# A ring of twenty weight buffers: the two that hold the normalized rows move from the ninth and tenth place to the nineteenth and twentieth

## The chip, the cores and the metric

The kernel runs on one core of one Trainium2 chip. The metric is the device time of one execution in microseconds (us); lower is better. The core's engines are PE (matrix products; PEld is its weight load), DVE (vector), ACT (scalar), POOL (GpSimd) and SP, which here only issues DMAs. Each engine works off its own list of instructions in order and waits on semaphores that other engines and landing DMAs raise.

## The reference, cut

An encoder layer on 512 rows of 1024 values: normalization, one projection, three groups of attention heads, an output projection with residual (`x` below), then a mixture of 32 experts. The part that matters here is the end:

```python
t = rms_norm(x, g_ffn)                        # the normalized rows, 512 x 1024
group = argmax(t @ w_r1 + b_r1)               # 1 of 4 groups
e0, e1 = top2((t @ w_r2 + b_r2)[group])       # 2 of its 8 experts, with gates
for every row and each of its two experts e:
    a = silu(t @ w1[e]) * (t @ w3[e])         # w1, w3: 32 x 1024 x 512
    y = a @ w2[e]                             # w2: 32 x 512 x 1024
    x += gate * y
```

Everything is float32. The three stacks of expert weights are 64 MiB each, 192 MiB in all, and the kernel reads every one of them once.

## The kernel before

**Stages.** By the profile's clock (us from the start of the span) the attention takes the time up to about 330. The output projection and the router follow: `route()` adds the residual (`x1`), normalizes it (`xr`, L1146), finds each row's experts, and makes one-hot tables that say which row goes to which slot of which expert. The experts run from 395 to the end, in 16 pairs `pr`: expert `pr` on 64 columns of PE, expert `pr + 16` on the other 64.

**The normalized rows.** `xr` lies in two buffers of 1 MiB, of the kinds `k0` and `va`, which attention has used before (L1144). ACT writes them row block by row block, stores each block to DRAM (`xd`, L1149), and PE reads them twice: for the first half of pair 0's gathered rows in `route()` (L1242), and for the second half in `gather_first` (L1389), which stands between the first two and the third of pair 0's products. Pairs 1 to 15 take their rows from `xd` by an indirect DMA that POOL issues (`rows_load`, L1361), two pairs ahead.

**The weights.** They come in 192 loads of 1 MiB, numbered 0 to 191 here, in the order in which PE uses them: per pair four of `w1`, four of `w3`, four of `w2` (names `w0_`, `w1_`, `w2_`; in pair 0 the order is `w1`, `w3`, `w1`, `w3` in twos). `load_w` (L926) takes the next one, picks a buffer, and puts a DMA on SP's list (L946 for `w1` and `w3`, L948 for `w2`). Load n waits until the readers of what lay in its buffer before are done. There are 20 buffers, in the order of `RING` (L36), and load n takes `RING[n % 20]`: so from load 20 on each load takes the place of the one 20 before it, and the first 20 take the places of things that attention or the router used:

- loads 0 to 7: `k2 b q k1 h h g g`
- loads 8 and 9: `k0` and `va`, the normalized rows
- loads 10 and 11: `m m`, the attention's output, read by the first half of the output projection
- loads 12 and 13: `h h`, split weights of the output projection (`wob`)
- loads 14 to 17: `d e j k`, laid where the other split weights (`wp`) and the rest of the attention's output (`mixb`) were
- loads 18 and 19: `v w`, laid where the router's temporaries (`val`, `tT`, `scr`) were

SP's list is worked off in order, so a load that waits holds all loads behind it. Beside its buffer, a load waits for the landing of an earlier DMA on the same one of eight semaphores (DMAHW0 to DMAHW7), which the stores of ACT share; this keeps about eight loads in flight.

**What sets the order around the change.** Calls of `load_w` are strewn through the program: eight loads late in the output projection (L1313, L1315), four behind `route()` (L1327), four when the `d e j k` buffers exist (L1334), two at L1449, then two in each half product (L1411) and in each half of the second product (L1502). Where a call stands sets only its place on SP's list; when it runs is set by what it waits for.

Of the kernel before, what the change touches and what calls it, by code (L numbers as in the profile page):

```python
# [32 lines left out]
F = 512  # L33
EPS = 1e-6
NEG = -1e30
RING = "k2 b q k1 h h g g k0 va m m h h d e j k v w".split()  # L36
LN_EXP = [s.name for s in SETS].index("natural_log_exp_and_others")

NA_KEYS = ((64, 248), (0, 248), (0, 248), (0, 192))
# [5 lines left out]
def tile_encoder(ctx: ExitStack, tc, x, mem, g_mix, g_mem, g_ffk, w_in, w_kv, w_out, gains,  # L45
# [35 lines left out]
    def granule(kind, name, dt=F32):  # L81
        return big.tile([P, 4, 512], dt, name=name, tag=kind, bufs=BUFS[kind])
# [17 lines left out]
    def pt(name):  # L100
        pts[0] += 1
        return bank("pt", NPT, name)
# [656 lines left out]
    def rows_turn(a):  # L759
        q = [bank(f"lg{j}", 1, "rT") if a % 2 else pt("rT") for j in range(2)]  # L760
        for k in range(KT):
            nc.tensor.transpose(q[k // 4][:, k % 4 * P:(k % 4 + 1) * P], x_sb[:, a, k * P:(k + 1) * P], ident)
        return q
# [109 lines left out]
    q = pt("warm")  # L873
# [12 lines left out]
    q = rows_turn(0)  # L886
# [32 lines left out]
    def rows_of(t):  # L919

        return t.rearrange("p (a b) c -> p a (b c)", b=2)

    def w2_rows(e):
        return w2[e].rearrange("(p k) c -> p k c", k=4)

    def load_w(count=1):  # L926
        for _ in range(count):
            n = loaded[0]
            if n >= len(order):
                return  # L930
            loaded[0] += 1
            pr, w, q, h = order[n]
            e = pr + 16 * h
            kind = RING[n % len(RING)]
            if kind in BUFS:
                t = granule(kind, f"w{w}_{e}_{q}")
            else:
                t = rings[kind].tile([P, 4, 512], F32, name=f"w{w}_{e}_{q}", tag="ring" + kind, bufs=RING.count(kind))
            wt[pr, w, q, h] = t
            if w == 1 and pr == NPAIR - 1 and q == 1:  # L940

                for k in (0, 2) if h else ():
                    for i in range(2):
                        nc.sync.dma_start(wt[pr, w, q, i][:, k:k + 2], w3[pr + 16 * i].rearrange("(p k) c -> p k c", k=KT)[:, 4 + k:6 + k, :])
            elif w < 2:
                nc.sync.dma_start(t, (w1, w3)[w][e].rearrange("(p k) c -> p k c", k=KT)[:, 4 * q:4 * q + 4, :])  # L946
            elif pr < NPAIR - 1:
                nc.sync.dma_start(rows_of(t), w2_rows(e)[:, 2 * q:2 * q + 2, :])  # L948
            elif n < len(order) - 2:
                nc.sync.dma_start(t, w2_rows(e)[:, :, q * 512:(q + 1) * 512])  # L950
            elif n == len(order) - 1:
                for f, c in ((slice(0, 4), 0), (slice(0, 2), 256), (slice(2, 4), 256)):
                    for i in range(2):
                        nc.sync.dma_start(wt[pr, w, q, i][:, f, c:c + 256], w2_rows(pr + 16 * i)[:, f, 512 + c:512 + c + 256])
# [346 lines left out]
    for n in range(2):  # L1301
        for a in range(4):
            def products():
                wo_products(a, n, (4, 5, 6, 7))
                join(wo_post(a, n, pos[n], False))

            def before():
                for w, k in (((1, 4 + a),), ((0, a), (1, a)))[n]:
                    wo_split(w, k)
                if a == 3 and n == 0:  # L1310
                    load_wo(1, 0)
                if a == 2 and n == 1:
                    load_w(4)  # L1313
                if a == 3 and n == 1:
                    load_w(4)  # L1315
            until(ready((4, 5, 6, 7)))
            step(products, before)
# [6 lines left out]
    until(lambda: not active)  # L1324
    assert not soft_q and not out_q
    route()
    load_w(4)  # L1327
    keep.close()
    moe = ExitStack()
    ring_ = moe.enter_context(tc.tile_pool(name="ringd", bufs=1, reuse_waits="tile"))  # L1330
# [240 lines left out]
    with tc.If(flag > 0):  # L1571
        with tc.tile_pool(name="ov", bufs=1) as ov, tc.tile_pool(name="ovps", bufs=1, space=PS) as ovs:
            with tc.For_i(0, NE) as e:
# [6 lines left out]
                for a in range(4):  # L1580
# [7 lines left out]
                    for k in range(KT):  # L1588
                        q = ovs.tile([P, P], F32, name="ovq1")
# [12 lines left out]
                    for f in range(4):  # L1602
                        q = ovs.tile([P, P], F32, name="ovq1")
# [76 lines left out]
```

## Time and profile before

| what | us |
|---|---|
| median of 3 runs | 896.99 (895.33 to 898.39) |
| the profiled execution | 897.9, of which the span is 896.1 |
| PE busy in the span | 823.3 (92%) |
| DVE, ACT, POOL busy | 421.1, 256.6, 149.9 |

The span reaches from the first to the last instruction; 1.8 us lie around it. PE is busy nearly all the time in attention and most of the time in the experts; what it waits for there is in the rows below. Times of loads and waits are of this one execution.

### The profile page before, as it was taken

Reading aid. Unit: us, or ns where it says so; the run is one execution under the profiler, and the core shown is the slowest. Engines: PE = TensorE matmul, PEld = TensorE weight load, DVE = VectorE, ACT = ScalarE, POOL = GpSimd, SP = SyncE. Lnnn points to the kernel's source line nnn. Section 1 sums busy time; section 2 is a strip of 40 time slices with the busy share of each in tenths; the row PEclk is TensorE's granted clock in tenths of the full one; section 3 lists DMA queues with packets and bytes.
Section 4 is the critical chain, followed back from the end, with each engine's and each line's share of the span. In section 5 each row is a group of like instructions: output and inputs, shape, how many; then the busy total and the mean of one; then the engine's idle time right before and its main releaser. Section 6 shows DMA issues by size and latency. Waiting matters only on the chain. (4 is left out here: it accounts for less than half of the span.)

```text
span 896.1 us, 12694 instructions
## 1 busy us (share of the span) xinstructions
PE 823.3 (92%) x4758; PEld 517.8 (58%) x4758; DVE 421.1 (47%) x1200; ACT 256.6 (29%) x768; POOL 149.9 (17%) x150
## 2 busy tenths in 40 slices
PE   8799999999899999989898889889988998899996
PEld 7789889889688767855244324333443343244433
DVE  6787795348678666551133213312331333033315
ACT  4667666664445533510000000000000100010010
POOL 5454222333323232130000000000000000000000
PEclk8999999999999999979999999999999999999998
DMA  9233121131312567116999999999999999999994
GB/s 326 51 94 102 52 91 50 48 115 48 95 44 92 133 227 304 72 50 244 423 403 427 426 425 425 427 426 426 427 426 426 425 426 426 426 427 426 426 407 155
DMA packets 66209, 243.54 MB, mean 272 GB/s; under 512 B 9498, under 2 KB 34074, under 8 KB 42336
## 3 DMA queue, kind: packets, MB, share of 16 engines
q1 hardware_dynamic: 55376, 230.18, 63.7%
q10 hardware_dynamic: 8608, 8.55, 3.4%
q0 software_dynamic: 2160, 3.96, 1.2%
q8 instruction: 39, 0.64, 0.3%
q14 instruction: 26, 0.21, 0.1%
HBM read 242.31 MB, written 4.26 MB: 275 GB/s over the span
## 5 line engine op out<-in xcount | busy, mean ns | idle before, releaser
L1408 PE MATMUL h<-w,xT 128*64 128x512 f32 x1024 | 248.2, 604 | 41.7 <-DMA w<-in_w_dram 40.2
L1408 PEld LDWEIGHTS h<-w,xT 128*64 128x64 f32 x1024 | 81.7, 138 | 203.1 <-issue 115.2
L1475 DVE TENSOR_TENSOR u<-u,h 128x512 f32<-128x512 f32 x16 | 11.0, 689 | 246.6 <-PE h L1408 246.6
L1494 PE MATMUL y<-w,uT 128*64 128x512 f32 x480 | 106.7, 595 | 0.7 <-ACT uT L1482 0.7
L189 POOL TENSOR_TENSOR wp<-wc,wp 128x512 fp32r<-128x512 f32 x51 | 67.0, 1318 | 129.9 <-ACT wp L188 104.1
L232 PE MATMUL pj<-wp,hTh 128*128 128x256 f32 (+1 forms) x268 | 79.3, 296 | 0.7 <-ACT hTh L776 0.7
L1361 POOL DMA_INDIRECT rows<-xd,where x15 | 15.1, 1009 | 381.0 <-PE uTp L1480 235.7
L233 PE MATMUL pj<-wp,hTh 128*128 128x256 f32 (+1 forms) x268 | 76.8, 287 | 0.8 <-POOL wp L189 0.8
L234 PE MATMUL pj<-wp,hTl 128*128 128x256 f32 (+1 forms) x268 | 76.7, 286 | 0.2 <-DVE hTl L779 0.2
L1426 DVE TENSOR_TENSOR x<-x,c 128x512 f32<-128x512 f32 x120 | 73.1, 682 | 2.8 <-PE c L1424 1.3
L1494 PEld LDWEIGHTS y<-w,uT 128*64 128x64 f32 x480 | 33.6, 137 | 65.8 <-issue 64.7
L1500 DVE SCALAR_TENSOR_TENSOR yl<-y,gate,yh 128x512 fp32r<-128x512 f32 x30 | 22.5, 750 | 80.8 <-ACT yh L1499 80.8
L1499 ACT ACTIVATE yh<-y,gate 128x512 fp32r<-128x512 f32 x30 | 20.6, 687 | 134.6 <-PE y L1494 133.5
L1482 ACT ACTIVATE uT<-uTp 128x512 f32<-128x512 f32 x16 | 9.6, 598 | 165.9 <-PE uTp L1480 165.9
L232 PEld LDWEIGHTS pj<-wp,hTh 128*128 128x128 f32 (+1 forms) x268 | 51.8, 193 | 3.7 <-issue 1.4
L233 PEld LDWEIGHTS pj<-wp,hTh 128*128 128x128 f32 (+1 forms) x268 | 51.8, 193 | 1.2 <-POOL wp L189 1.2
L234 PEld LDWEIGHTS pj<-wp,hTl 128*128 128x128 f32 (+1 forms) x268 | 51.7, 193 | 0.4 <-DVE hTl L779 0.4
L1464 ACT ACTIVATE u<-h 128x512 f32<-128x512 f32 x16 | 9.6, 597 | 140.8 <-PE h L1408 140.8
L1423 PE MATMUL c<-yh,ot 128*128 128x512 f32 x120 | 48.2, 402 | 0.0
L1424 PE MATMUL c<-yl,ot 128*128 128x512 f32 x120 | 46.9, 391 | 0.0
L232 PE MATMUL pj<-wq,hTh 128*128 128x256 f32 (+1 forms) x124 | 37.4, 301 | 2.8 <-ACT raw L279 2.8
L234 PE MATMUL pj<-wq,hTl 128*128 128x256 f32 (+1 forms) x124 | 35.6, 287 | 0.0
(319 smaller groups left out, 1440.9 us busy)
## 6 DMA issues: line engine op xcount, KB each, us to landing
w<-in_w_dram SPq DMA_DIRECT2D x188, 1024.0 KB, 19.6
wc<-in_w_in_dram SPq DMA_DIRECT2D x15, 1024.0 KB, 5.2
wo<-in_w_out_dram SPq DMA_DIRECT2D x4, 1024.0 KB, 5.0
w<-in_w_dram SPq DMA_DIRECT2D x6, 512.0 KB, 10.8
wc<-in_w_kv_dram SPq DMA_DIRECT2D x2, 1024.0 KB, 9.0
x<-in_x_dram ACTq DMA_DIRECT2D x4, 512.0 KB, 8.4
xd<-xr ACTq DMA_DIRECT2D x4, 512.0 KB
nab<-in_na_tab_dram ACTq DMA_DIRECT2D x8, 248.0 KB
```

The costliest lines, as they stand in the source:

```text
L189: (eng or nc.gpsimd).tensor_sub(dst[1], src, dst[0])
L232: nc.tensor.matmul(o, th, self.hi[k], start=(k == 0), stop=False)
L233: nc.tensor.matmul(o, th, self.lo[k], start=False, stop=False)
L234: nc.tensor.matmul(o, tl, self.hi[k], start=False, stop=(k == KT - 1))
L1361: nc.gpsimd.indirect_dma_start(out=rows_in[pr % 2], out_offset=None, in_=xd, in_offset=bass.IndirectOffsetOnAxis(ap=where_[:, pr:pr + 1], ...
L1408: nc.tensor.matmul(p[h * 64:(h + 1) * 64, :], xT[k // 4][:, k % 4, h * 64:(h + 1) * 64], wt[pr, w, q, h][:, k % 4, :], start=(k == 0), sto ...
L1423: nc.tensor.matmul(c, ot[:, a], yh, start=True, stop=False)
L1424: nc.tensor.matmul(c, ot[:, a], yl, start=False, stop=True)
L1426: V.tensor_add(sl, sl, c)
L1494: nc.tensor.matmul(y[h * 64:(h + 1) * 64, :], uT[:, f, h * 64:(h + 1) * 64], rows_of(wt[pr, 2, q, h])[:, f % 2, n * 512:(n + 1) * 512], st ...
L1499: nc.scalar.activation(yh, y, AF.Copy, scale=gate[:, pr:pr + 1])
L1500: V.scalar_tensor_tensor(yl, y, gate[:, pr:pr + 1], yh, op0=ALU.mult, op1=ALU.subtract)
```

## The change

The ring's order for loads 0 to 17 skips `k0` and `va`; they come as loads 18 and 19. From load 20 on the order repeats with a period of 20 as before, so each load still takes the buffer of the one 20 before it. The call behind `route()` puts two loads instead of four on SP's list.

```diff
-RING = "k2 b q k1 h h g g k0 va m m h h d e j k v w".split()
+RING = "k2 b q k1 h h g g m m h h d e j k v w".split()
+AGAIN = ["k0", "va"] + RING
...
-            kind = RING[n % len(RING)]
+            kind = RING[n] if n < len(RING) else AGAIN[(n - len(RING)) % len(AGAIN)]
...
     route()
-    load_w(4)
+    load_w(2)
```

The line numbers behind the first hunk grow by one (L948 becomes L949). SP's list, loads 8 to 19, before; in brackets the semaphores each waits for: PE_49, DVE_49, Activation_49 and Pool_49 are raised by the engines, DMAHWn_49 by landings. The first two rows are `k0` and `va`, the next two `m m`, then `h h`, `d e j k`, `v w`:

```order
L948 DMA w2_0_0_4995<-in_w2_dram 128x2048 [waits DMAHW2_49,DMAHW1_49,DMAHW5_49,PE_49,Activation_49]
L948 DMA w2_16_0_4997<-in_w2_dram 128x2048 [waits DMAHW4_49,DMAHW3_49,DMAHW6_49,PE_49,Activation_49]
L948 DMA w2_0_1_4999<-in_w2_dram 128x2048 [waits DMAHW7_49]
L948 DMA w2_16_1_5001<-in_w2_dram 128x2048 [waits DMAHW0_49]
L946 DMA w0_1_0_5011<-in_w1_dram 128x2048
L946 DMA w0_17_0_5013<-in_w1_dram 128x2048
L946 DMA w0_1_1_5015<-in_w1_dram 128x2048 [waits DVE_49]
L946 DMA w0_17_1_5017<-in_w1_dram 128x2048 [waits DMAHW5_49,DVE_49]
L946 DMA w1_1_0_5063<-in_w3_dram 128x2048 [waits DMAHW6_49]
L946 DMA w1_17_0_5065<-in_w3_dram 128x2048 [waits DMAHW7_49]
L946 DMA w1_1_1_5077<-in_w3_dram 128x2048 [waits DVE_49,DMAHW0_49,Activation_49,Pool_49]
L946 DMA w1_17_1_5079<-in_w3_dram 128x2048 [waits DMAHW1_49]
```

The same place in the changed kernel. The loads are the same, the buffers are not: the first two rows are now `m m`, then `h h`, `d e j k`, `v w`, and the last two are `k0` and `va`:

```order
L949 DMA w2_0_0_4995<-in_w2_dram 128x2048 [waits DMAHW2_49,DVE_49]
L949 DMA w2_16_0_4997<-in_w2_dram 128x2048 [waits DMAHW3_49]
L949 DMA w2_0_1_5007<-in_w2_dram 128x2048 [waits DMAHW4_49,PE_49]
L949 DMA w2_16_1_5009<-in_w2_dram 128x2048 [waits DMAHW5_49,PE_49]
L947 DMA w0_1_0_5011<-in_w1_dram 128x2048 [waits DMAHW7_49,DVE_49,PE_49]
L947 DMA w0_17_0_5013<-in_w1_dram 128x2048 [waits DMAHW1_49,DVE_49,PE_49]
L947 DMA w0_1_1_5059<-in_w1_dram 128x2048 [waits DMAHW2_49,PE_49]
L947 DMA w0_17_1_5061<-in_w1_dram 128x2048 [waits DMAHW3_49,PE_49]
L947 DMA w1_1_0_5073<-in_w3_dram 128x2048 [waits DVE_49,PE_49,DMAHW5_49,Activation_49,Pool_49]
L947 DMA w1_17_0_5075<-in_w3_dram 128x2048 [waits DMAHW6_49,PE_49]
L947 DMA w1_1_1_5085<-in_w3_dram 128x2048 [waits DMAHW7_49,PE_49]
L947 DMA w1_17_1_5087<-in_w3_dram 128x2048 [waits DMAHW4_49,DMAHW0_49,PE_49]
```

What moved is the pair of waits on `xr`'s readers: from the head of this list to its end. Before, the ten loads behind it need hardly any wait of their own, because the wait at the head covers them; now each names the engine that last read its buffer.

The lists of PE, DVE, ACT and POOL hold the same instructions in the same order. On ACT, around the stores of the second and third block of `xr`, only semaphores differ. Before:

```order
L1149 DMA xd_61<-xr_4621 128x1024 [waits DMAHW2_49]
L1213 ACTIVATE scr_4726<-scr_4726 128x1 [waits DVE_49]
L1146 ACTIVATE xr_4769<-x1_4034,rst_4045 128x1024 [waits DVE_49]
L1149 DMA xd_61<-xr_4769 128x1024 [waits DMAHW3_49,Activation_49]
L1105 ACTIVATE junk_4784,sqs_4046<-x1_4034 128x512 [waits DVE_49]
```

And in the changed kernel:

```order
L1150 DMA xd_61<-xr_4621 128x1024 [waits DMAHW6_49]
L1214 ACTIVATE scr_4726<-scr_4726 128x1 [waits DVE_49]
L1147 ACTIVATE xr_4769<-x1_4034,rst_4045 128x1024 [waits DVE_49]
L1150 DMA xd_61<-xr_4769 128x1024 [waits DMAHW0_49,Activation_49]
L1106 ACTIVATE junk_4784,sqs_4046<-x1_4034 128x512 [waits DVE_49]
```

The stores stand where they stood; they share semaphores with other loads now (loads 5 and 7 here, load 10 for the fourth block), whose landing they wait for.

## Rows read from the trace of the kernel before

**Rows 1.** The page's span in 40 equal slices of 22.4 us: the busy share of the DMA engines in tenths, and GB/s moved.

```profile
DMA  9233121131312567116999999999999999999994
GB/s 326 51 94 102 52 91 50 48 115 48 95 44 92 133 227 304 72 50 244 423 403 427 426 425 425 427 426 426 427 426 426 425 426 426 426 427 426 426 407 155
```

**Rows 2.** SP's own waits between 326 and 480 us, longest first: line, what it waited for, us in total, times, longest.

```profile
SPq L948 <- PE xTp L1389: 36.2, 2, 35.7
SPq L948 <- DMA xd<-xr: 27.9, 1, 27.9
SPq L948 <- DMA gov<-wkb: 14.5, 1, 14.5
```

**Rows 3.** SP's timeline between 325 and 450 us: start, length of the merged stretch, issues in it.

```profile
326.62 20.81 SPq L946 DMA_DIRECT2D w<-in_w_dram  x8
411.09 2.29 SPq L948 DMA_DIRECT2D w<-in_w_dram  x4
413.43 12.79 SPq L946 DMA_DIRECT2D w<-in_w_dram  x8
429.03 19.61 SPq L948 DMA_DIRECT2D w<-in_w_dram  x4
```

**Rows 4.** Stretches of time: length, busy us of PE, PEld, DVE, ACT, POOL (instructions), granted clock of PE as a share of full, DMA share, GB/s.

```profile
354.00:358.00 4.00, 4.00 (x23) 2.81 (x22) 1.24 (x4) 0.84 (x3) 0.00 (x0) 1.00 0.99 412
358.00:362.00 4.00, 4.00 (x19) 3.29 (x18) 1.83 (x8) 2.08 (x5) 0.00 (x0) 1.00 0.07 29
366.00:370.00 4.00, 4.00 (x27) 3.48 (x24) 1.39 (x7) 2.45 (x7) 0.00 (x0) 1.00 0.00 0
406.00:410.00 4.00, 4.00 (x19) 4.00 (x18) 0.00 (x0) 0.00 (x0) 0.00 (x0) 1.00 0.00 0
414.00:418.00 4.00, 4.00 (x16) 1.18 (x14) 0.00 (x0) 0.00 (x0) 0.00 (x0) 0.76 1.01 422
440.00:480.00 40.00, 34.64 (x156) 13.51 (x156) 8.92 (x15) 2.57 (x4) 0.99 (x1) 1.00 1.00 412
520.00:560.00 40.00, 37.23 (x168) 14.70 (x166) 10.37 (x16) 3.94 (x6) 0.99 (x1) 1.00 1.01 426
```

**Rows 5.** The page's list of DMA issues: engine, count, KB each, median us from issue to landing.

```profile
w<-in_w_dram SPq DMA_DIRECT2D x188, 1024.0 KB, 19.6
```

**Rows 6.** Who last uses the memory of each later buffer: PE's and DVE's timelines between 342 and 396 us (start, us, line, operation, out<-in). In order: the last product that reads `mixm`, the last that reads `wob`, the last of three listed blocks of products that read `wp` and `mixb`, DVE's last `val`, and PE's last reading of it.

```profile
342.77 0.39 PE L1296 MATMUL wop<-wob,mixm 128*128 128x512 f32 x1
362.35 0.39 PE L1296 MATMUL wop<-wob,mixb 128*128 128x512 f32 x1
365.07 0.39 PE L1296 MATMUL wop<-wp,mixb 128*128 128x512 f32 x1
369.15 0.40 PE L1296 MATMUL wop<-wp,mixb 128*128 128x512 f32 x1
375.00 0.40 PE L1296 MATMUL wop<-wp,mixb 128*128 128x512 f32 x1
392.40 0.48 DVE L1235 TENSOR_SCALAR val<-places,scr 128x128 fp32r<-128x128 f32 x2
394.16 0.60 PE L1250 MATMUL tb<-val 128*128 128x48 f32 x2
```

**Rows 7.** PE's timeline, pair 0 up to the first products of pair 1 (in brackets the idle time before, and what ended it).

```profile
404.07 7.89 PE L1389 MATMUL xTp<-G,xr 128*128 128x128 f32 x32
412.74 8.66 PE L1408 MATMUL h<-w,xT 128*64 128x512 f32 x32 [0.78 <-DVE xT L1345]
421.33 1.15 PE L1397 MATMUL xTp<-ident,rows 128*128 128x128 f32 x8
423.73 7.09 PE L1494 MATMUL y<-w,uT 128*64 128x512 f32 x32 [0.69 <-ACT uT L1482]
430.64 4.45 PE L1408 MATMUL h<-w,xT 128*64 128x512 f32 x18
```

**Rows 8.** PE's timeline, one later pair from its turning of rows (480.38) to the next pair's (510.46).

```profile
480.38 1.16 PE L1397 MATMUL xTp<-ident,rows 128*128 128x128 f32 x8
485.66 7.09 PE L1494 MATMUL y<-w,uT 128*64 128x512 f32 x32
492.58 8.19 PE L1408 MATMUL h<-w,xT 128*64 128x512 f32 x34
502.01 3.65 PE L1408 MATMUL h<-w,xT 128*64 128x512 f32 x16 [1.25 <-DMA w<-in_w_dram]
506.88 3.65 PE L1408 MATMUL h<-w,xT 128*64 128x512 f32 x14 [1.21 <-DMA w<-in_w_dram]
510.46 1.16 PE L1397 MATMUL xTp<-ident,rows 128*128 128x128 f32 x8
```

**Rows 9.** PE's waits from 395 us to the end (us in total, times, longest), and from PE's timeline the last of them.

```profile
PE h L1408 <- DMA w<-in_w_dram: 40.2, 37, 1.4
...
864.32 7.08 PE L1408 MATMUL h<-w,xT 128*64 128x512 f32 x30 [0.90 <-DMA w<-in_w_dram]
```

**Rows 10.** The small transfers beside the loads: ACT's last store of `xr`, POOL's first row gather, and of all 15 gathers the us from issue to landing.

```profile
383.10 0.33 ACTq L1149 DMA_DIRECT2D xd<-xr  x1
396.61 1.23 POOL L1361 DMA_INDIRECT rows<-xd,where  x1 [6.19 <-issue]
DMA to landing us min/median/max: 4.0/8.0/9.1
```

## The prediction

> **What bounds the kernel now.** I read the page's slices of DMA first [rows 1]. From the twentieth slice to the last but one the DMA engines are full, at 425 to 427 GB/s in nearly every slice: the experts' stage is paced by the weights. Just before it lies a hole: two slices at 72 and 50 GB/s, in a kernel that has all its weights in DRAM from the start. The stretches of 4 us show its edges: full at 354 to 358, nothing at 358 to 362, still nothing at 406 to 410, full at 414 [rows 4]. Then I asked why SP issues nothing there. Its timeline has eight loads by 347.4 (326.62 + 20.81) and the next one at 411.09 [rows 3]; its waits name the reason: 27.9 us for the stores of `xr`, then 35.7 us for PE's last reading of `xr` in `gather_first` [rows 2]. Load 8 wants `k0`, and ten loads that want other buffers stand behind loads 8 and 9.
>
> PE in the experts' stage is the engine that waits. One pair takes 510.46 - 480.38 = 30.1 us, with two visible waits for weights, 1.25 and 1.21 us [rows 8]; over the stage they are 37 waits and 40.2 us, the last at 864.32 [rows 9]. So PE alone would need 30.1 - 2.5 = 27.6 us a pair, and the weights' pace decides until 864; behind that, 31.8 us to the end of the span hold the last products and the stores.
>
> **What one load costs.** 1024 KB are 1.0486 MB [rows 5]; at 426 GB/s [rows 4] that is 2.46 us of all DMA engines. The median of 19.6 us from issue to landing [rows 5] is eight of these, the eight in flight. The Trainium skill, page "DMA: Bandwidth & Descriptors", section Specifications, gives about 358 GB/s as what HBM grants one core; by it a load would take 2.93 us, an estimate, and the ten loads below 29.3 instead of 24.6 us, for 867.7 us. The slices here run at 426 GB/s for 400 us [rows 1], so on this core the measurement decides.
>
> **The change, part by part.** It removes nothing and adds nothing: 192 loads, the same order of weights, the same 20 buffers, and the other engines' lists are unchanged. It only takes two waits away from ten loads. When each can now go, from the last user of its buffer [rows 6]:
>
> - loads 8 and 9 (`m m`): the readers are done at 343.2, before load 7 is issued; so right behind it, at about 347.5.
> - loads 10 and 11 (`h h`): 362.35 + 0.39 = 362.7.
> - loads 12 and 13 (`d e`): 365.5 and 369.6. Loads 14 and 15 (`j k`): by 375.4.
> - load 16 (`v`): 392.9. Load 17 (`w`): 394.8.
> - loads 18 and 19 (`k0 va`): as load 8 before, at 411.1.
>
> All waits on landings in that list are for DMAs issued at least 8 us earlier. The engines are otherwise nearly idle there, so the eight loads up to 375.4 have landed well before 390, and the last two by 394.8 + 2 x 2.46 and a few us, some 402. At 411.1, when the stream starts without a break, 18 loads are in, where 8 were before. What is left is **ten loads less: 10 x 2.46 = 24.6 us of DMA time**.
>
> Does the stream keep going from there? At 411.1 loads 18 to 23 go at once, since their buffers were read by 404 (loads 0 to 3 are used before `gather_first` starts at 404.07 [rows 7]); that is 6 x 2.46 = 14.8 us of transfer, until 426. Loads 24 to 27 take the buffers of the products that run from 412.74 to 421.3, loads 28 to 31 those of 423.73 to 430.6 [rows 7]: each is free before the stream needs it. Later PE frees 12 buffers in 27.6 us, faster than 12 x 2.46 = 29.5 fill. With ten loads landed and unread of 20, the others are in flight or in use; the ring holds the lead. One wait moves: the store `gov` held load 22 for 14.5 us [rows 2]; it now holds load 32. Fourteen loads stand between 411 and it in both orders (8 to 21, 18 to 31), so the dip it leaves, 412 instead of 426 GB/s in 40 us [rows 4], 40 x (1 - 412/426) = 1.3 us, stays; at best it goes.
>
> **What becomes of the lead.** Pair 0 has no wait for weights before and none after [rows 7], so PE reaches 430.64 as before. From there it runs its own pace: 27.6 instead of 30.1 us a pair, 40.2 / 15 = 2.7 us won per pair, until it has eaten the lead: 24.6 / 2.7 = 9.2 pairs, at about 430.6 + 9.2 x 27.5 = 684. From there on the weights pace it again, 24.6 us earlier than before, and the last wait at 864.3 comes at 839.7. The 31.8 us behind it do not change. PE has 40.2 us of waits to give, more than the 24.6, so DMA stays the bound, and 15.6 us of waits remain. Sum, on the profiled execution: 897.9 - 24.6 = 873.3, span 871.5; it stood 0.9 above the median, so from the median 896.99 - 24.6 = **872.4**.
>
> **What I cost at nothing, and its cover.** The hole is also where the router works, and loads now run beside its small transfers. ACT's four stores of `xr` stand in the middle of ACT's list; the last, at 383.10 [rows 10], now waits for load 10, issued 20 us earlier. The gathers of rows take 4.0 us in an empty stretch and up to 9.1 beside the stream [rows 10]. The first is issued at 396.61 and its rows are turned at 421.33 [rows 7, 10]: 24.7 us, of which 9.1 leave a cover of 15.6. The Trainium skill, same page, section Queues, rings and completion order, says that each DMA engine takes turns between the queues, packet by packet, so a small transfer is slowed but not put behind the whole stream; the 9.1 against 4.0 agrees. No row prices what a transfer that I have not named (the program's own code comes by DMA too) would lose on PE's path here: from nothing, since PE stays at 4.00 of 4.00 us busy beside the loads at 354 to 358 [rows 4], to 9.1 - 4.0 = 5.1 us if one such step lands on the path. I take nothing, the nearer row, and keep 5.1 for the range. PE's clock is at full, 2.4 GHz, in the stretches of the experts' stage [rows 4], and with fewer waits nothing speaks for less.
>
> **The rivals.**
> - *The router's stage stretches.* Loads beside it slow a chain of two or more transfers on the path to `gather_first`; 411.1 moves by that much, and the stream's restart with it, one for one. Two steps: 2 x 5.1 = 10.2 us, 882.6. Against it: the stores and gathers that I can name have 15 us of cover.
> - *PE becomes the bound.* The 2.5 us of visible waits a pair may stand in part for something PE must do anyway. Above (411.1 to 864: 15 pairs) 30.1 - 24.6 / 15 = 28.5 us a pair PE decides; at 29.0 only 15 x 1.1 = 16.5 us come back, 880.5. Against it: pair 0's sixteen-product halves run at 3.65 us each without a gap, as do the later ones [rows 8].
> - *It doesn't do what it says.* The ten loads find another wait that lasts until 411, say load 8 itself; nothing behind it moves and the time stays 897. Against it: the list of waits, where loads 8 to 15 name only things that are over by 375.4.
> - *Slower than before.* The gathers for pair 1 starve behind the loads. Each us past the cover of 15.6 stops PE at 421.33 and stops the freeing of buffers with it; to undo the gain as well, the rows would have to land 15.6 + 24.6 = 40 us late. At 46 us late the time is 903. Against it: beside the full stream the worst of 15 gathers took 9.1 us [rows 10].
>
> **How the numbers follow.** Chances: forecast 0.81, stretched stage 0.08, PE as bound 0.06, nothing moves 0.03, slower 0.02. The range takes the forecast with its open ends: down 1.3 (the dip of `gov` goes) and 1.5 (the runs lie within 895.33 to 898.39), 869.6; up 5.1 (one step on the path) and 1.5, 879.0. What lies outside, most of the first three rivals, is under 2 in 10. This kernel's measurement can tell 0.3%, 2.7 us, from no change: faster 0.95, same 0.03, slower 0.02.
>
> **What the changed profile would show.** Right: SP issues ten loads between 347 and 395, in groups at about 347, 363 to 375 and 393 to 395; its wait for PE's reading of `xr` shrinks to some 16 us; the two empty slices carry 10.5 MB more; PE has no wait for weights from 395 to about 680, and 15.6 us of them in all; the last one is at about 840. Wrong: `gather_first` begins later than 404 (stretched stage); PE's pairs take over 28.5 us without waits, and the DMA rate falls below 426 because SP waits for PE (PE bound); no issue of SP before 411 (nothing moves); PE stands before L1398 at 421 (the gathers).

## The result, and the profile after

The changed kernel took 871.53, 874.41 and 875.60 us, median 874.4; the kernel before, run beside it, 897.7 (895.33 to 899.5). The ratio is 0.9736, with a 95% interval of 0.9694 to 0.9777: 23.7 us less (20.0 to 27.5). A fourth execution of the changed kernel took 2013.48 us, which no other run repeated and nothing here explains; it is left out of the ratio.

The profiled execution took 871.5, its span is 869.7. The page's slices, which are 21.7 us long now; against [rows 1] most of the hole has filled:

```profile
DMA  9233113123121267964999999999999999999994
GB/s 319 70 97 106 50 50 99 49 70 97 49 79 62 85 187 301 409 237 163 426 416 425 427 425 425 425 427 427 426 427 426 425 427 426 426 427 427 425 402 138
```

Where two slices stood at 72 and 50 GB/s, the three from 348 to 413 us now carry 409, 237 and 163, at the cost of none behind them: from the twentieth on it is 416 to 427 again, up to the last two. A short hole is left, in this stretch (columns as in [rows 4]):

```profile
405.00:410.00 5.00, 5.00 (x23) 5.00 (x22) 0.00 (x0) 0.00 (x0) 0.00 (x0) 1.00 0.00 0
```

Some of SP's waits between 326 and 480 us (line, what it waited for, total, times, longest) and its timeline from 324 to 413 (start, length, issues), against [rows 2, 3]:

```profile
SPq L947 <- DVE val L1236: 17.1, 1, 17.1
SPq L947 <- PE xTp L1390: 16.5, 2, 16.0
SPq L949 <- DMA gov<-wkb: 14.2, 1, 14.2
SPq L949 <- PE wop L1297: 13.4, 2, 12.5
SPq L947 <- DMA xd<-xr: 2.8, 1, 2.8
```

```profile
324.74 20.91 SPq L947 DMA_DIRECT2D w<-in_w_dram  x8
345.75 15.57 SPq L949 DMA_DIRECT2D w<-in_w_dram  x4
363.71 46.97 SPq L947 DMA_DIRECT2D w<-in_w_dram  x8
410.74 2.18 SPq L949 DMA_DIRECT2D w<-in_w_dram  x4
```

Where SP stood from 347.4 to 411.1, twelve further loads are issued. Narrower windows of the same timeline show them one by one: two from 345.8, six between 359.6 and 374.0, two from 391.3 to 393.3, and at 409.4 the two that take `xr`'s place. SP's wait for `gather_first` is 16.0 us at the longest instead of 35.7, and that for the `xr` stores 2.8 instead of 27.9; its longest single wait is now the 17.1 us for `val`, whose place load 16 takes.

PE's timeline in the experts' stage (start, length, line, operation, count, idle time before it), first pair 0, then some of the later pairs and the last wait:

```profile
402.44 7.89 PE L1390 MATMUL xTp<-G,xr 128*128 128x128 f32 x32
411.11 8.73 PE L1409 MATMUL h<-w,xT 128*64 128x512 f32 x32 [0.79 <-DVE xT L1346]
419.77 1.16 PE L1398 MATMUL xTp<-ident,rows 128*128 128x128 f32 x8
...
470.04 1.16 PE L1398 MATMUL xTp<-ident,rows 128*128 128x128 f32 x8
...
482.25 13.90 PE L1409 MATMUL h<-w,xT 128*64 128x512 f32 x64
496.08 1.16 PE L1398 MATMUL xTp<-ident,rows 128*128 128x128 f32 x8
...
574.35 1.16 PE L1398 MATMUL xTp<-ident,rows 128*128 128x128 f32 x8
...
586.53 8.15 PE L1409 MATMUL h<-w,xT 128*64 128x512 f32 x34
595.90 3.65 PE L1409 MATMUL h<-w,xT 128*64 128x512 f32 x16 [1.23 <-DMA w<-in_w_dram]
600.84 3.65 PE L1409 MATMUL h<-w,xT 128*64 128x512 f32 x14 [1.28 <-DMA w<-in_w_dram]
...
816.27 1.15 PE L1398 MATMUL xTp<-ident,rows 128*128 128x128 f32 x8
...
837.27 7.08 PE L1409 MATMUL h<-w,xT 128*64 128x512 f32 x30 [0.93 <-DMA w<-in_w_dram]
```

```profile
PE h L1409 <- DMA w<-in_w_dram: 22.8, 21, 1.3
```

The second block is PE's waits from 395 us to 897. Against [rows 8, 9]: a pair that waits for no weights runs from 470.04 to 496.08, 26.0 us; the first wait is at 595.9, and from there on the pairs look as they did before. 22.8 us of visible waits are left of 40.2, and the last ends at 837.3 instead of 864.3.

**A caution for reading these times.** The start of the stage moves between executions for reasons outside the change: load 0 is issued at 326.62 in the profile before and at 324.74 here, and attention has no changed instruction ahead of it. So I compare the experts' stage by its own length, from the start of `gather_first` to the end of the span: before, 896.1 - 404.07 = 492.0 us; after, 869.7 - 402.44 = 467.2 (here and below the last digit is that of the unrounded span). That is 24.8 us less, by one execution of each. The experiments below are read by this length, with the ratio of the times beside it.

A second thing moves by itself. The 32 products behind `gather_first` take 8.66 us in the profile before [rows 7] and 8.73 here, because the clock granted to PE falls there to 0.50 of full, its lower level of 1.2 GHz, for some 3 us; ahead of them PE turned rows at full clock and then idled for 0.8 us. In the first run of experiment 3 and in the last of experiment 7 they take 8.78; in the other nine profiles they take 7.09 at full clock, behind the same idle time. One kernel shows both (experiment 3), so this isn't what the change does. It makes a stage up to 1.7 us longer where PE or the buffers it frees decide the end.

### The profile page after: what moved, and what is told of

It is laid out like the page before. It is cut to its first block, busy times and chain, and to the rows that moved or that the text cites. A ratio compares the mean times of both kernels' runs of the same rounds, so it can differ in the third digit from the quotient of the medians.

```text
span 869.7 us, 12699 instructions
## 1 busy us (share of the span) xinstructions
PE 813.8 (94%) x4758; PEld 514.4 (59%) x4758; DVE 420.9 (48%) x1200; ACT 256.4 (29%) x768; POOL 149.7 (17%) x150
## 5 line engine op out<-in xcount | busy, mean ns | idle before, releaser
L1409 PE MATMUL h<-w,xT 128*64 128x512 f32 x1024 | 239.5, 603 | 24.2 <-DMA w<-in_w_dram 22.8
L1409 PEld LDWEIGHTS h<-w,xT 128*64 128x64 f32 x1024 | 79.5, 138 | 178.9 <-issue 127.5
```

Of the source, the lines that this page charges most:

```text
L1409: nc.tensor.matmul(p[h * 64:(h + 1) * 64, :], xT[k // 4][:, k % 4, h * 64:(h + 1) * 64], wt[pr, w, q, h][:, k % 4, :], start=(k == 0), sto ...
```

## The experiments

Line numbers are those of each kernel. "Stage" is the length just defined; 492.0 is that of before, 467.2 that of after.

**1. Only two loads ahead.** In the kernel before, only `m m` pass the normalized rows.

```diff
-RING = "k2 b q k1 h h g g k0 va m m h h d e j k v w".split()
+RING = "k2 b q k1 h h g g m m k0 va h h d e j k v w".split()
```

> The order of before with the buffers of the normalized rows two places later, as loads 10 and 11 (only m m go ahead of them). Theory (lead): each load that is in before the stream starts at 411 us is worth 2.46 us at the end; two loads, 4.9 us off the 897.2 of before, so 892.3. Rival (threshold): the gain comes only when pair 1 has its weights early and PE runs through the first pairs without a stop; both loads here belong to pair 0, which never waited, so 897.

SP's timeline:

```profile
344.91 65.82 SPq L948 DMA_DIRECT2D w<-in_w_dram  x4
410.78 9.03 SPq L946 DMA_DIRECT2D w<-in_w_dram  x8
```

Median 891.9 against 896.0, ratio 0.9949 (0.9929 to 0.9970); stage 890.2 - 402.44 = 487.8, 4.2 less. The group of four starts at 344.9 and is not through until 410.7: two loads go, the third stands. Even two loads ahead show in the time, and the interval leaves out 1, as the single loads would have it and a threshold would not.

**2. Eight loads ahead.** All but `v w` pass, with two loads instead of four behind `route()`.

```diff
-RING = "k2 b q k1 h h g g k0 va m m h h d e j k v w".split()
+RING = "k2 b q k1 h h g g m m h h d e j k k0 va v w".split()
...
-    load_w(4)
+    load_w(2)
```

> The buffers of the normalized rows as loads 16 and 17: m m h h d e j k go ahead, v w stay behind. Theory (lead): eight loads, 8 x 2.46 = 19.7 us, 877.5, two loads (4.9 us) short of the changed kernel. Rival (threshold): pair 1 has its first four loads early; if that is enough the time is the changed kernel's, 872 to 875, and if not it is near 897.

877.2 against 896.0, ratio 0.9772 (0.9746 to 0.9798); stage 876.3 - 403.9 = 472.4, 19.6 less, where eight loads of 2.46 us are 19.7.

**3. Fourteen loads ahead, and again.** On the changed kernel: after the first 18 loads the ring goes round, and `k0 va` come as loads 22 and 23, so four more loads pass them.

```diff
-AGAIN = ["k0", "va"] + RING
+AGAIN = "k2 b q k1 k0 va h h g g m m h h d e j k v w".split()
```

> The buffers of the normalized rows as loads 22 and 23: in the changed order k2 b q k1 go ahead of them a second time, since PE has read these by about 398 and 402 us, ahead of gather_first. Theory (lead): fourteen loads in by 411, four more than the changed kernel, 4 x 2.46 = 9.8 us, 865; PE has 22.8 us of waits left in the changed kernel to pay for it. If the ring is full then and SP waits for PE's buffers, 2 to 4 us of it are lost, 867 to 869. Rival (threshold): pair 1 is supplied already; nothing more, 874.

868.1 against 896.0, ratio 0.9674 (0.9650 to 0.9697); stage 867.1 - 405.05 = 462.0, 30.0 less. Fourteen loads would be 34.4. Stretches of 4 us (length, busy us of PE, PEld, DVE, ACT, POOL, granted clock, DMA share, GB/s) and SP's waits between 395 and 480 us show where the rest went:

```profile
406.00:410.00 4.00, 4.00 (x19) 4.00 (x18) 0.00 (x0) 0.00 (x0) 0.00 (x0) 1.00 1.02 430
418.00:422.00 4.00, 4.00 (x22) 1.29 (x18) 0.00 (x0) 0.60 (x1) 0.00 (x0) 1.00 0.71 227
446.00:450.00 4.00, 3.42 (x20) 2.72 (x19) 3.56 (x6) 0.60 (x1) 0.99 (x1) 1.00 0.65 210
450.00:454.00 4.00, 4.00 (x20) 1.97 (x21) 3.68 (x6) 0.00 (x0) 0.00 (x0) 1.00 0.91 357
```

```profile
SPq L947 <- PE h L1409: 14.5, 3, 6.1
SPq L949 <- DMA gov<-wkb: 12.3, 1, 12.3
SPq L947 <- PE y L1495: 11.0, 3, 5.1
```

The stretch that was empty in [rows 4], 406 to 410, is full. But the stream then dips at 418 and at 446 to 454. By now the ring is full: SP waits for products to free buffers, and at 446 for the store `gov`, with too little in flight behind it. So the gain falls short of 2.5 us a load where the twenty buffers end. The same kernel run a second time:

> Fourteen ahead once more, beside the run with gov on POOL on the same chip: 868.

866.7 against 897.3, ratio 0.9668 (0.9645 to 0.9691); stage 863.5 - 402.83 = 460.6. It has PE at full clock behind `gather_first` and the first run has not, which fits the 1.4 us between them: with the ring full, products that end later free their buffers later.

**4. Ten loads left out of the kernel before.** In five pairs, 8 to 12, ACT fills half of `w2` (two of its four loads) with zeros instead, ten loads in all; the ring and its stall stay.

```diff
+            if w == 2 and q == 0 and 8 <= pr < 13:
+                nc.scalar.activation(t..., iota.unsqueeze(1).to_broadcast([P, 16, P]), AF.Copy, scale=0.0)
-            if w == 1 and pr == NPAIR - 1 and q == 1:
+            elif w == 1 and pr == NPAIR - 1 and q == 1:
```

> The kernel before, where ten of the 192 loads (half of w2 in pairs 8 to 12) are left out and ACT fills their buffers with zeros, so ten half products have no weights and the output lacks their part. The empty stretch before 411 stays as it was. Theory (the stream's bytes behind 411 set the end): 24.6 us less, 872.6, as in the changed kernel. Rival (the gain comes from the empty stretch itself or the router's stage, not from the bytes behind it): 897, or 898 with ACT's ten fills of about 2 us.

SP's timeline still has the hole, from 345.5 to 411.8:

```profile
325.01 20.46 SPq L948 DMA_DIRECT2D w<-in_w_dram  x8
411.80 2.44 SPq L950 DMA_DIRECT2D w<-in_w_dram  x4
```

872.3 against 896.0, ratio 0.9721 (0.9695 to 0.9746); stage 871.6 - 404.78 = 466.8, 25.2 less. Ten loads that aren't there are worth what ten loads sent early are worth (24.8): what the change gives is transfer time behind 411, not anything that an earlier start does to the router.

**5. Twenty loads left out of the changed kernel.** The same edit with `3 <= pr < 13`, to see what is left when weights no longer pace PE.

> The changed kernel, where twenty of the 192 loads (half of w2 in pairs 3 to 12) are left out and ACT fills their buffers with zeros; the output lacks their part. The stream then needs 10 x 2.46 = 24.6 us a pair there and PE is the only bound up to the last pairs. It asks how much waiting PE really has left. If the visible waits of the changed kernel (22.8 us) are all: 875 - 22.8 = 852. If a pair without waits takes the 26.1 us that the changed kernel shows between 456 and 482 us, against 30.1 at the stream's pace, then about 8 pairs x 4.0 = 32 us are left: 843.

Two stretches (columns as above), and from PE's timeline the 32 products behind `gather_first` and the first and last turning of rows of twelve pairs:

```profile
480.00:600.00 120.00, 120.00 (x572) 49.86 (x568) 36.96 (x58) 30.23 (x29) 3.98 (x4) 1.00 1.01 426
700.00:800.00 100.00, 100.00 (x480) 43.28 (x478) 33.95 (x54) 11.10 (x16) 2.00 (x2) 1.00 1.01 421
```

```profile
412.20 7.09 PE L1411 MATMUL h<-w,xT 128*64 128x512 f32 x32 [0.78 <-DVE xT L1348]
...
470.14 1.16 PE L1400 MATMUL xTp<-ident,rows 128*128 128x128 f32 x8
...
782.92 1.16 PE L1400 MATMUL xTp<-ident,rows 128*128 128x128 f32 x8
```

835.7 against 897.3, ratio 0.9320 (0.9305 to 0.9336); stage 833.5 - 403.52 = 430.0. PE is busy throughout both stretches and has no wait for weights at all; a pair takes (782.92 - 470.14) / 12 = 26.07 us. Both my numbers for it, 852 from the visible waits and 843 from a pair of 26.1, were too high. The eight pairs that I counted were right: in the changed kernel those from 574.35 to 816.27 take 241.9 us, 33.4 more than eight take here. What I left out of the 467.2 - 430.0 = 37.2 is 2.8 us behind the last turning of rows (53.4 there, 50.6 here) and 1.0 ahead of 470, where the changed kernel's profile has the lower clock. If weights never kept PE waiting, the time would be about 836, an estimate from this run.

**6. The store `gov` on POOL's queue.** The store that held SP for 14.2 us shares its semaphore with loads when ACT issues it; here POOL does, and in all four runs with it there SP's waits no longer name `gov`.

```diff
-        nc.scalar.dma_start(gov.rearrange("(a p) e -> p a e", p=P), wkb[:, 0])
+        nc.gpsimd.dma_start(gov.rearrange("(a p) e -> p a e", p=P), wkb[:, 0])
```

On fourteen ahead (experiment 3), twice:

> Fourteen ahead as before, and the store gov issued by POOL instead of ACT, so that it shares no semaphore with the loads and SP does not wait 12.3 us for it. In the run with fourteen ahead the DMA engines are then at 0.65 and 0.91 in 446 to 454 us, some 1.8 us lost. Theory (lead): 1.5 to 2 us off that run, 866. Rival (the ring is what is full there, PE's buffers decide, not SP's wait): no change, 868.

> Fourteen ahead with gov on POOL once more, on the chip of the two others: 863.

And on the changed kernel:

> The changed kernel with gov issued by POOL. The dip at the store (422 instead of 426 GB/s over 440 to 480 us in the changed kernel) is 0.4 us: 874 to 875, no difference that can be measured.

With fourteen ahead 862.8 (ratio 0.9625, 0.9608 to 0.9643, stage 458.5) and 864.7 (0.9649, 0.9632 to 0.9667, stage 457.7); the second dip is gone:

```profile
446.00:454.00 8.00, 8.00 (x38) 3.49 (x38) 4.44 (x8) 0.47 (x1) 0.00 (x0) 1.00 1.01 426
```

That is 2 to 4 us of stage against experiment 3 (462.0 and 460.6; 2.1 and 2.9 against the second, which has PE at full clock as these have), and on each chip the times of the two kernels don't overlap or hardly do: 862.3 to 865.9 against 863.7 to 871.4, and 863.5 to 866.0 against 867.1 to 868.9. On the changed kernel 872.4 (0.9725, 0.9710 to 0.9739), stage 872.3 - 405.48 = 466.8: no difference to 467.2.

**7. The order of before, but the two waiting loads on another list.** The ring of before is untouched; ACT issues loads 8 and 9.

```diff
-                nc.sync.dma_start(rows_of(t), w2_rows(e)[:, 2 * q:2 * q + 2, :])
+                (nc.scalar if n in (8, 9) else nc.sync).dma_start(rows_of(t), w2_rows(e)[:, 2 * q:2 * q + 2, :])
```

> The ring's order of before, untouched, but the two loads that wait for the normalized rows (8 and 9) are issued by ACT, whose list has nothing to do between its table load at 391 us and 418 us. Theory (a blocked list): what cost the time is not the order of the buffers but that eighteen... ten and more free loads stood behind two blocked ones on SP's list; with these gone SP can issue loads 10 to 23 by 402, fourteen ahead, as in the runs with fourteen ahead: 867 to 868. Rival (the order in the ring itself, or which weights come when, makes the gain): 897, or slower, since pair 0's second product needs loads 8 and 9 at 422 and they come in beside the stream.

SP's timeline, and behind it ACT's:

```profile
344.96 0.90 SPq L948 DMA_DIRECT2D w<-in_w_dram  x2
358.86 33.69 SPq L946 DMA_DIRECT2D w<-in_w_dram  x8
398.04 4.24 SPq L948 DMA_DIRECT2D w<-in_w_dram  x4
```

```profile
408.35 1.29 ACTq L948 DMA_DIRECT2D w<-in_w_dram  x2
409.67 1.28 ACT L1464 ACT_TABLE_LOAD   x1 [20.88 <-PE xTp L1389]
```

862.9 against 895.7, ratio 0.9626 (0.9598 to 0.9653); stage 861.6 - 401.38 = 460.2. SP is through with fourteen loads by 402.3, while the two that need `xr`'s place leave ACT at 408.4, as late as ever. The buffers and their order are those of before; only the list on which the two stand has changed. So the loss lay in the list, not in the ring. ACT's list is held in its turn: the table load behind the two ran at 391.37 before and runs at 409.67 here, still ahead of its first use at 413.78. The second form, with `gov` on POOL as well:

> The same with the store gov issued by POOL: as the run with fourteen ahead and gov on POOL, 863.

866.3 (0.9663, 0.9642 to 0.9683), stage 461.5: here moving `gov` gains nothing. The traces tell this from the ring's order. With the loads on ACT's list SP waits 9.6 us for `gov` instead of 12.3, and there is no second dip for the move to fill. The same stretch, first in 7, then in the second run of 3:

```profile
442.00:450.00 8.00, 6.70 (x30) 3.60 (x30) 5.88 (x10) 0.60 (x1) 0.64 (x1) 1.00 1.01 423
442.00:450.00 8.00, 7.34 (x38) 4.72 (x38) 7.33 (x12) 0.60 (x1) 0.99 (x1) 1.00 0.84 314
```

That the second form has even 1.3 us more of stage fits its lower clock behind `gather_first`, which the first does not have.

## Why the prediction was right, and where a step was off

**The bound and the price of a load: right.** The stage by the number of loads ahead of the two: none 492.0, two 487.8, eight 472.4, ten 467.2, fourteen 460.6 and 462.0. Up to ten that is 2.1 to 2.5 us a load, against the 2.46 of the prediction, and leaving loads out instead (experiment 4) gives the same. The Trainium skill, page "DMA: Bandwidth & Descriptors", section Specifications, has about 358 GB/s as the limit of one core (a stack's 716 over two cores); by it ten loads would be worth 29.3 us, an estimate. The stage lost 24.8, so the slices' 426 GB/s decide here.

**What holds the loads: right.** SP's longest wait for `xr`'s readers became 16.0 us ("some 16"), the ten loads went ahead of that wait, between 345.8 and 393.3, and experiment 7 shows the cause by itself: the wait at the head of an in-order list.

**What was costed at nothing: right.** From load 0 to the start of `gather_first` it is 404.07 - 326.62 = 77.45 us before and 402.44 - 324.74 = 77.70 after: the router's stage did not stretch. In the eleven other profiles this length lies between 77.0 and 79.9, and it is 79.8 with the order of before (experiment 4), so a stretch of up to 3 us could not be told from scatter. All 15 gathers landed within 4.8 to 8.7 us, the first is issued at 394.84, and PE turns its rows at 419.77 without a wait. `gov` holds SP 14.2 us, with a dip to 422 GB/s in 440 to 480, milder than the 412 of before; it stayed, and experiment 6 on the changed kernel shows that it is worth nothing there.

**What becomes of the lead: the mis-sized term.** The prediction took PE's own pace as 30.1 less the visible waits, 27.6 us a pair, so the lead would last 9.2 pairs, to 684, and leave 15.6 us of waits. A pair without waits takes 26.0 us, so a pair at the weights' pace waits some 4.1 us, not 2.5; the lead lasts about 24.6 / 4.1 = 6 pairs, and PE's first wait came at 595.9. 22.8 us of visible waits are left, where experiment 5 ends 37.2 earlier. The missing part sits in stretches that the trace shows as busy: 64 products take 13.9 us without a wait, but 510.46 - 492.58 = 17.88 in [rows 8], of which only 2.46 are shown idle. [rows 8] could have told: its 32 products `y`, of the same shape and without a wait, take 7.09 us. The whole stage has 492.0 - 430.0 = 62.0 us more than experiment 5, 1.6 of them by the lower clock, where [rows 9] shows 40.2 in 37 waits: the other 20 are some 0.55 us per wait. That a lone product's modelled end covers this much of the gap behind it would fit, but wasn't shown. The error did not touch the total, since the weights decide the end either way; had the lead been over 40.2 us, it would have: I would have put the floor some 20 us too high.

**The rivals.** A stretched router's stage and starving gathers are refuted by the numbers above (two steps would have been 10.2 us, outside the scatter; the gathers had 15 us to spare), "nothing moves" by SP's timeline. PE as the bound needed over 28.5 us a pair; it is 26.0. (What the prediction held against it, sixteen products of pair 0 in 3.65 us, is in no row: [rows 7] has 32 in 8.66, and the 3.65 of [rows 8] stand behind waits.) None of the runs made the small transfers late on purpose, so the point at which the slower case would set in was not tried. PE's clock was not at full in every stretch of [rows 4], as the prediction reads it: 414 to 418 has 0.76. The 32 products there slow down before and after alike, so the total is left alone.

**What is left to gain.** The versions with fourteen ahead, by the ring (experiments 3 and 6) or by ACT's list (experiment 7), lie at ratios of 0.9625 to 0.9674, some 6 to 10 us below the changed kernel (0.9736 of 897). Part of this is the hole that the change leaves, with nothing moved from 405 to 410. The change puts the two loads at the end of the first twenty, but four more buffers are free before `gather_first` ends. Further than that the twenty buffers don't reach.

## What to carry to other kernels

When the transfers are the bound and their rate falls to nothing somewhere, look first at what stands at the head of the issuing engine's list: one load that waits for a late buffer holds every free one behind it, and each held load costs its whole transfer time at the end. Cure it by order or by another list, and count the gain in loads until the ring is full. Do not read an engine's own pace as the time less its visible waits; find a stretch without any wait, or make one.

## What the runs showed that I had not expected

- Visible waits of PE for weights were two thirds of the real ones: 40.2 us shown, some 60 gone once weights no longer paced it.
- Two loads that wait on ACT's list for their buffer until 408.4 cost nothing that the stage shows (460.2 against 460.6 and 462.0 by the ring's order).
- With the stream sent into the router's stage, the loads moved at up to 409 GB/s in a slice beside the small transfers there, and `gather_first` still began 77.70 us after load 0, against 77.45.
